# Gates and first key blocks as two threads, wider margins, and a solve whose loads are issued from two queues

## The chip, the cores and the metric

The kernel runs on one core of a Trainium2 chip, in one launch. Its time is what the device takes for it, in microseconds (us). A core has five engines with a queue of instructions each, worked off in order: TensorE (PE in the profile; its weight loads are PEld), VectorE (DVE), ScalarE (ACT), GpSimd (POOL) and SyncE (SP). SP and ACT also issue DMA transfers here (SPq and ACTq). An engine waits for another through semaphores. [...]

## What is computed

One layer of a hybrid model is applied to 128 context tokens and 512 latent tokens (640 in all, 2048 channels). With the parts that this change doesn't touch cut:

```
h    = rms_norm(x) * (1 + scale) + shift        # scale, shift from c @ w_mod
proj = h @ w_in                                 # u_f, z_f, q, k, v, z_d, a, b
y_f  = fft(u_f).real * silu(z_f)                # Fourier group
q, k, v = silu(short_conv(qkv))                 # 12 heads of 128
log_g = -exp(a_log) * softplus(a + dt_bias);  beta = sigmoid(b)     # the gates
per head, direction (2) and chunk of tokens:
  A    = I + strict_lower(beta * k @ k.T * exp(g_i - g_j))
  Tinv = triangular inverse of A
  scan over chunks:  v_new = Tinv @ (beta v - beta exp(g) k @ S)
                     o     = exp(g) q @ S + tril(q @ k.T * decay) @ v_new
                     S     = exp(g_last) S + (k * decay).T @ v_new
y = concat(y_f, rms_norm(o) * silu(z_d)) @ w_out;   out = rms_norm(x + gate * y)
```

Outputs are both token streams and the scan states of the context.

## The kernel before

**The stream.** The projection is cut into tiles of 128 output columns (53 of them in the main stream: u, k, v, q, z, f). Each tile is two halves of 320 tokens by 16 blocks of 128 channels, and each of these products is taken in three passes of rounded high and low parts (L1360: h_hi by whi, h_lo by whi, h_hi by wlo), so a tile is 96 matmuls. Weights come in as `raw` (issued by ACT, L1327), are rounded by ACT to `whi` (L1336), and POOL forms the rest `wlo` (L1344). At the end comes the output projection (L1628) in the same manner.

**The heads.** Beside the stream each of the 12 heads passes through generators: `conv` (L752 to L761 give KT, vT, QT), `blocks` (k transposed at L775 inside `to_tokens`; k times k at L841; the copies kkd at L846; the decays `gr`, loaded at L816 from gb4, L852 to L860; the store of `pd`, L863), `solve` (the 16x16 and 32x32 inverses of A on VectorE: loads NP, L875; steps L885, L887, L898, L900; store xd, L907; loads DD and DP, L912 and L915; a transpose L918; matmuls L929 and L940), `decay` (gb, L961; L973 to L980), `prep` (L1012, copy YT at L1014, L1025, L1040, L1047), `scan` (L1072 to L1125 and the squares L1137) and `head_out` (L1154). `gates` (L637 on) computes decays and betas of all heads once, from a load `abT`, and stores them to gd and gb4. `shifts` adds what the shift vector contributes: its last part (L617 and L620) runs over weight tiles wm that are loaded for it alone. `res_gates` forms column sums of two more weight groups on VectorE out of loads `gw` (L1258, steps L1264 and L1266 in `rows256`); the first two of these groups end in L1278.

**What sets the order.** The instructions are written in an order that a planner picks while the kernel is built. It keeps an estimate `est` of when each engine becomes free and when each tile is written, and all the generators above as threads with a rank. A thread stops at `yield`, and says when it wants to go on:

```
t = x.when + (GUARD if "P" in x.on else -LEAD)
return max([t] + [est.free[engine[e]] - SLACK for e in x.on if e != "P"])
```

`yield "P", t` goes on when TensorE's estimated time has reached t + 0.3, `yield "V"`, `"A"` or `"S"` when the thread's last result is due within 0.4 us and that engine is free within 0.9; a bare `yield` is "P" with the thread's own last end. `yield "poll"` waits until something is in the set `done`. In between, the stream's matmuls fill TensorE, two blocks of channels at a time, in the order of the list `names`; tile k or q of head h may only be finished once the scan of head h - 2 is done. The planner's times set the order alone; on the chip every engine runs as its semaphores let it.

`all_blocks` runs `gates()` first and then `blocks(0)`, `blocks(1)` and so on, as one thread.

Of the kernel before, what the change touches and what calls it, by code (L numbers as in the profile page):

```python
# [9 lines left out]
F32 = mybir.dt.float32  # L10
# [7 lines left out]
P = 128  # L18
# [194 lines left out]
def hybrid_step(ctx: ExitStack, tc: tile.TileContext, x_prompt, x_sample, state_ctx, c, c_ctx,  # L213
# [4 lines left out]
    est = Estimate()  # L218
# [26 lines left out]
    gb4 = dram.tile([NH, 4, 2, 160], F32, name="gb4")  # L245
# [332 lines left out]
    def shifts():  # L578
# [32 lines left out]
        for c in range(4):  # L611
            while len(sh_in) < n + 2:
                yield "poll"
            yield "P", max(est.written(x) for x in sh_in[n:n + 2]) + 1.7
            for j in range(4):
                x = sh_in[n + j // 2]
                PE.matmul(pc[32 * j:32 * j + 32, 0:384], lhsT=csh[:, 4 * c + j, :],  # L617
                          rhs=x[:, 0:768].rearrange("p (i n) -> p i n", i=3)[:, :, P * (j % 2):P * (j % 2) + P],
                          start=c == 0, stop=c == 3, tile_position=(0, 32 * j))
                PE.matmul(pa[32 * j:32 * j + 32, 0:48], lhsT=csh[:, 4 * c + j, :], rhs=x[:, 768 + 48 * (j % 2):816 + 48 * (j % 2)],  # L620
                          start=c == 0, stop=c == 3, tile_position=(0, 32 * j))
            n += 2
            sh_used[0] = n
# [13 lines left out]
    def gates():  # L637
# [20 lines left out]
        ACT.activation(beta, pbv[:, 24:48, :], AF.Tanh, scale=0.5)  # L658
        DVE.tensor_scalar(beta, beta, 0.5, 0.5, ALU.mult, ALU.add)
        DVE.tensor_scalar(nbeta, beta, -1.0, None, ALU.mult)  # L660
        DVE.tensor_scalar(aa, ax, -1.0, None, ALU.mult)
        DVE.tensor_tensor(aa, ax, aa, ALU.min)
        ACT.activation(aa, aa, AF.Exp)
# [147 lines left out]
    def blocks(h):  # L811
        s = st_h[h]
        KT = s["KT"]
        gr = g.tile([P, 2, 5, 32], F32, tag="gr", name="gr", bufs=1)
        for b in range(4):
            SP.dma_start(out=gr[32 * b:32 * b + 32].rearrange("p d t c -> p d (t c)"), in_=gb4[h, b].partition_broadcast(32))  # L816
        s["k"] = k = g.tile([P, 5, P], F32, tag="k", name="k", bufs=2)
        for sl, pv, n in to_tokens(KT):
            ACT.copy(k[:, sl, :], pv)
# [8 lines left out]
        rk2 = g.tile([P, 5], F32, tag="rk2", name="rk2", bufs=2)  # L828
        POOL.tensor_tensor(nk, sk, K("phalf")[:, 0:5], ALU.pow)
        DVE.reciprocal(rk2, sk)  # L830
        for nm, src in (("s3", beta4), ("ns3", nbeta4)):
            s[nm] = g.tile([P, 2, 5], F32, tag=nm, name=nm, bufs=3)
            DVE.tensor_tensor(s[nm], src[:, :, h, :], rk2.unsqueeze(1).broadcast_to([P, 2, 5]), ALU.mult)
# [14 lines left out]
        for b in range(4):  # L848
            POOL.memset(KK[32 * b:32 * b + 32, :, :, 32 * b:32 * b + 32], 0.0)
        done.add(("kk", h))  # L850
        sh = [P, 2, 5, 32]
        DVE.tensor_tensor(gr, gr, gg4[:, :, h, :].unsqueeze(3).broadcast_to(sh), ALU.subtract)  # L852
        DVE.tensor_tensor(gr, gr, dmask.unsqueeze(2).broadcast_to(sh), ALU.add)
# [14 lines left out]
    def solve(h):  # L868
# [3 lines left out]
        for b in range(4):  # L872
            for q in range(2):
                r = 32 * b + 16 * q
                SP.dma_start(out=NP[10 * b:10 * b + 10, 272 * q:272 * q + 256].rearrange("u (r c) -> u r c", r=16),  # L875
                             in_=pd[r:r + 16, :, :, 16 * q:16 * q + 16].rearrange("r d t c -> (d t) r c"))
        yield "V"
        tmp = g.tile([40, 768], F32, tag="tmp", name="tmp", bufs=1)
# [26 lines left out]
            yield "V" if q == 0 else "S"  # L905
        xd = dram.tile([40, 32, 32], F32, tag="xd", name="xd", bufs=2)
        SP.dma_start(out=xd, in_=X2)  # L907
        yield "S"
        while h and ("dd", h - 1) not in done:
            yield "poll"  # L910
        for b in range(4):
            SP.dma_start(out=DD[32 * b:32 * b + 32, 0:2].rearrange("p d t c -> p (d t) c"),  # L912
                         in_=xd[10 * b:10 * b + 10].rearrange("u r c -> r u c"))
            o = 32 * (b ^ 1)
            SP.dma_start(out=DP[o:o + 32], in_=xd[10 * b + 5:10 * b + 10].rearrange("u r c -> r u c"))  # L915
        yield "V", est.written(DD) + 1.5
        f2, N = "p d t c -> p (d t c)", s["N"]
        DVE.transpose(DD[:, 2:4].rearrange(f2), DD[:, 0:2].rearrange(f2))  # L918
        yield
        while h and ("prep", h - 1) not in done:  # L920
            yield "poll"

# [7 lines left out]
                              start=True, stop=True, tile_position=(32 * b, o))  # L930
        for j in range(2):
            ACT.copy(M2[:, j].rearrange(f1), px[j][:, 0:160])
        yield
        px = [bank(), bank()]
        for t in range(5):
            for j in range(2):
# [317 lines left out]
    def rows256(src, by):  # L1254
        x = g.tile([P, 4, 256], F32, tag="gw", name="gw", bufs=1)
        gw, acc = x[:, 0:2], x[:, 2:4]
        for j in range(NK // 2):
            SP.dma_start(out=gw, in_=src[:, 2 * j:2 * j + 2])  # L1258
            yield "V", est.last + 1.0
            for q in range(2):  # L1260
                for m in range(2):
                    one = by[:, 2 * j + q, m:m + 1]
                    if j + q:
                        DVE.scalar_tensor_tensor(acc[:, m], gw[:, q], one, acc[:, m], ALU.mult, ALU.add)  # L1264
                    else:
                        DVE.tensor_scalar(acc[:, m], gw[:, q], one, None, ALU.mult)  # L1266
        yield
        return x

    def shift_u():  # L1270
# [32 lines left out]


    place = {"k": C_K, "v": C_V, "q": C_Q, "z": C_ZD, "u": 0, "f": 512}
    names = "u0 u1 u2 u3 k1 q1 v1 z0 z1 f0".split()
    fill = {2: "", 3: "z2 f1", 11: "f2 z10 f3 z11"}
    for h in range(2, NH):
        names += [f"k{h}", f"v{h}", f"q{h}"] + fill.get(h, f"z{h - 1}").split()
    tiles = [(n[0], int(n[1:]), place[n[0]] + P * int(n[1:])) for n in names]  # L1310
# [8 lines left out]
    def loads():  # L1319
        for n, parts in enumerate(jobs):  # L1320
            while n >= len(ready) // 2 + 2:
                yield "poll"
            if n > 1:
                yield "A", est.freed(raws[n - 2])
            raw = wpool.tile([P, 8, P], F32, tag="raw", name="raw", bufs=2)
            for sl, src in parts:
                ACT.dma_start(out=raw[:, sl].rearrange("p a b -> p (a b)") if len(parts) > 1 else raw, in_=src)  # L1327
            raws.append(raw)

    def casts():  # L1330
        for c in range(2 * len(jobs)):
            while c >= 2 * len(raws) or c >= used[0] + 5:
                yield "poll"
            yield "A", max(est.written(raws[c // 2]), est.freed(his[c - 5]) if c > 4 else 0.0)
            his.append(wpool.tile([P, 4, P], F32R, tag="whi", name="whi", bufs=5))
            ACT.copy(his[c], raws[c // 2][:, 4 * (c % 2):4 * (c % 2) + 4])  # L1336
# [94 lines left out]
    fconst = []  # L1431

    def all_blocks():
        yield from gates()
        for h in range(NH):
            while ("k", h) not in done:
                yield "poll"
            yield from blocks(h)
            done.add(("blocks", h))
# [7 lines left out]

    def decays():
        for h in range(NH):
            while not {("v", h), ("q", h), ("kk", h)} <= done:  # L1450
                yield "poll"
            yield from decay(h)
            yield
            done.add(("decay", h))
# [204 lines left out]
    main, tail = stream(), out_stream()  # L1659
    est.free.update(PE=13.0, Activation=8.0, DVE=8.0, Pool=5.0, SP=0.0)  # L1660
    nc.push_inst_callback(est)
    for rank, steps in ((0, loads()), (0, casts()), (0, lows()), (2.4, solves()), (2.2, all_blocks()), (2, scans()), (3, outs()), (4, preps()), (5, decays()),
                        (2.5, fouriers(0)), (2.5, fouriers(1)), (10, res_gates()), (0.5, shift_loads()), (0.6, shifts()), (2.7, load_y(0)), (2.7, load_y(1))):
        begin(rank, steps)
    for i, kind in enumerate("kvq"):
# [41 lines left out]
```

## Time and profile before

| | |
|---|---|
| median of 3 runs | 1441.15 us (1438.79 to 1443.88) |
| the profiled execution | 1442.66 us, its span 1440.9 us |
| TensorE busy | 1373.0 us, 95% |
| TensorE weight loads | 1267.6 us, 88% |
| VectorE, ScalarE, GpSimd busy | 58%, 47%, 44% |
| mean granted TensorE clock | 0.982 |
| chain that ended last | TensorE 55%, VectorE 17%, DMA 4% of the span |

A share of busy time is a mean over stages. What an instruction waited for is read from the lists of waits and from the timeline, where the bracket behind a row gives the idle time before it and the engine and instruction that ended it.

### The profile page before, as it was taken

The numbers are of one execution on the slowest core, as the hardware profiler recorded it, in microseconds if no ns is written. First come the engines' busy times: TensorE is split into PE (matmuls) and PEld (weight loads), VectorE is DVE, ScalarE is ACT, GpSimd is POOL, SyncE is SP. The second block draws the span as 40 slices with busy tenths as digits, with TensorE's granted clock in tenths as the row PEclk, the third lists the DMA queues.
The fourth block names the chain that finished last, engine by engine and source line by source line (L and its number), as shares of the span: only waits on it lengthen the run. The fifth ranks groups of instructions, "written<-read, shape, count | busy, mean of one in ns | idle before, by whom it ended". The sixth has DMA issues, their size and how long they took to land.

```text
span 1440.9 us, 31437 instructions
## 1 busy us (share of the span) xinstructions
PE 1373.0 (95%) x12284; PEld 1267.6 (88%) x12284; DVE 842.6 (58%) x1756; ACT 670.8 (47%) x1808; POOL 628.4 (44%) x649
## 2 busy tenths in 40 slices
PE   6999989888999999999999999999999999999996
PEld 4799869887999999898999999998989998888884
DVE  5441127878597858586685969676755635322024
ACT  5332226644555464544455564645555544423134
POOL 2233213353355455354453545444454432346375
PEclk9999999898999999999999999999999999999998
DMA  9988973353344434334443424433333445594003
GB/s 311 277 262 265 309 191 106 95 144 100 90 129 116 117 101 127 103 110 124 117 125 101 127 79 133 120 113 113 97 93 88 137 138 164 172 338 147 30 0 146
DMA packets 271057, 203.71 MB, mean 141 GB/s; under 512 B 55801, under 2 KB 241094, under 8 KB 270782
## 3 DMA queue, kind: packets, MB, share of 16 engines
q1 hardware_dynamic: 148286, 129.88, 29.3%
q10 hardware_dynamic: 122624, 71.84, 17.5%
q8 instruction: 97, 1.59, 0.4%
q14 instruction: 50, 0.41, 0.1%
HBM read 177.67 MB, written 23.99 MB: 140 GB/s over the span
## 4 chain that ended last, share of the span: by engine, by line
PE 55%; DVE 17%; DMA 4%; ACT 2%; issue 2%; SPq 2%; POOL 1%; ACTq 0%; DVEq 0%; POOLq 0%
PE mbank L1360 28%; PE bank L1628 8%; PE mbank L1628 7%; DVE tmp L898 3%; DVE gw L1264 3%; DVE tmp L885 2%; PE bank L1091 1%; PE bank L1111 1%; PE bank L1099 1%; PE bank L1072 1%; DMA DD<-xd 1%; PE bank L1079 1%; DVE XB L887 1%; PE bank L841 1%; DVE YB L900 1%
## 5 line engine op out<-in xcount | busy, mean ns | idle before, releaser
L1360 PE MATMUL mbank<-h_hi,whi 128*128 128x320 f32 (+1 forms) x1696 | 554.3, 327 | 0.0
L1344 POOL TENSOR_TENSOR wlo<-raw,whi 128x512 fp32r<-128x512 f32 x232 | 329.6, 1426 | 506.8 <-ACT whi L1336 452.2
L1360 PE MATMUL mbank<-h_lo,whi 128*128 128x320 f32 (+1 forms) x1696 | 528.3, 311 | 0.0
L1360 PE MATMUL mbank<-h_hi,wlo 128*128 128x320 f32 (+1 forms) x1696 | 528.0, 311 | 0.1
L1360 PEld LDWEIGHTS mbank<-h_hi,whi 128*128 128x128 f32 x1696 | 322.5, 190 | 10.7 <-issue 7.4
L1360 PEld LDWEIGHTS mbank<-h_lo,whi 128*128 128x128 f32 x1696 | 322.7, 190 | 0.1
L1360 PEld LDWEIGHTS mbank<-h_hi,wlo 128*128 128x128 f32 x1696 | 322.2, 190 | 0.3 <-POOL wlo L1344 0.3
L1336 ACT CAST whi<-raw 128x512 fp32r<-128x512 f32 x232 | 142.2, 618 | 195.2 <-PE mbank L1360 141.6
L1264 DVE SCALAR_TENSOR_TENSOR gw<-gw,cz 128x256 f32<-128x256 f32 x240 | 130.6, 602 | 5.6 <-DMA gw<-in_w_mod 5.4
L283 POOL TENSOR_TENSOR wlo<-raw,whi 128x512 fp32r<-128x512 f32 (+1 forms) x44 | 55.3, 1267 | 86.8 <-ACT whi L282 64.9
L1628 PE MATMUL mbank<-wlo,y_hi 128*128 128x512 f32 x160 | 63.8, 399 | 2.6 <-POOL wlo L283 2.0
L1628 PE MATMUL mbank<-whi,y_hi 128*128 128x512 f32 x160 | 64.1, 401 | 0.0
L1628 PE MATMUL mbank<-whi,y_lo 128*128 128x512 f32 x160 | 64.0, 400 | 0.0
L1628 PE MATMUL bank<-whi,y_lo 128*128 128x512 f32 x160 | 63.2, 395 | 0.0
L1628 PE MATMUL bank<-wlo,y_hi 128*128 128x512 f32 x160 | 63.1, 394 | 0.0
L1628 PE MATMUL bank<-whi,y_hi 128*128 128x512 f32 x160 | 62.9, 393 | 0.0
L1094 ACT ACTIVATE vn<-bank,s 128x128 f32<-128x128 f32 x120 | 37.6, 366 | 50.0 <-PE bank L1091 49.5
L977 ACT ACTIVATE E<-gb,ngg 128x128 f32<-128x128 f32 x120 | 41.7, 396 | 32.6 <-DVE AT L980 25.4
L282 ACT CAST whi<-raw 128x512 fp32r<-128x512 f32 (+1 forms) x44 | 24.6, 579 | 56.4 <-PE bank L1628 19.1
L965 POOL TENSOR_TENSOR gb<-gb,cst 128x640 f32<-128x640 f32 x24 | 37.0, 1558 | 27.7 <-DMA gb<-gd 27.7
L1084 POOL TENSOR_SCALAR kd<-k,edl 128x128 f32<-128x128 f32 x96 | 46.4, 497 | 1.1 <-PE bank L1099 0.7
L1106 DVE SCALAR_TENSOR_TENSOR S<-S,egl,bank 128x128 f32<-128x128 f32 x72 | 21.6, 339 | 37.9 <-PE bank L1099 35.8
(334 smaller groups left out, 2452.6 us busy)
## 6 DMA issues: line engine op xcount, KB each, us to landing
raw<-in_w_in ACTq DMA_DIRECT2D x106, 512.0 KB
wm<-in_w_mod SPq DMA_DIRECT2D x64, 512.0 KB
gw<-in_w_mod SPq DMA_DIRECT2D x64, 256.0 KB
raw<-in_w_out ACTq DMA_DIRECT2D x48, 256.0 KB
gb<-gd SPq DMA_DIRECT2D x12, 640.0 KB
yd<-zs SPq DMA_DIRECT2D x16, 320.0 KB
yt<-yd SPq DMA_DIRECT2D x16, 320.0 KB
out<-res SPq DMA_DIRECT2D x10, 512.0 KB
```

The source lines that it names most:

```text
L283: sub.tensor_tensor(wlo, raw_part, whi, ALU.subtract)
L885: DVE.tensor_tensor(tv, NPd[:, :, i, 0:i].unsqueeze(2).broadcast_to(s4), Xd[:, :, 0:i, 0:i].rearrange("p h j c -> p h c j"), ALU.mult)
L898: DVE.tensor_tensor(tv, A.unsqueeze(2).broadcast_to(s4), B.rearrange("p j c -> p c j").unsqueeze(1).broadcast_to(s4), ALU.mult)
L965: POOL.tensor_tensor(gv, gv, masks[d].unsqueeze(1).broadcast_to([P, 5, P]), ALU.add)
L977: ACT.activation(E[:, 1 - d], gb[:, d, P * t:P * (t + 1)], AF.Exp, bias=ngg4[:, d, h, t:t + 1])
L1084: POOL.tensor_scalar(kd[:, d], k[:, tt[d], :], edl4[:, d, h, tt[d]:tt[d] + 1], 1.0, ALU.mult, ALU.mult)
L1094: ACT.mul(vn[:, d], pv[:, P * d:P * (d + 1)], s["s3"][:, d, tt[d]:tt[d] + 1])
L1264: DVE.scalar_tensor_tensor(acc[:, m], gw[:, q], one, acc[:, m], ALU.mult, ALU.add)
L1336: ACT.copy(his[c], raws[c // 2][:, 4 * (c % 2):4 * (c % 2) + 4])
L1344: POOL.tensor_tensor(lo, raws[c // 2][:, 4 * (c % 2):4 * (c % 2) + 4], his[c], ALU.subtract)
L1360: PE.matmul(pm[:, 0:b - a], lhsT=w, rhs=h[k][:, a:b], start=k + m == 0, stop=k == NK - 1 and m == 2)
L1628: PE.matmul(acc[t], lhsT=a[kk][:, sl], rhs=w, start=kk == order[0] and j == 0, stop=kk == order[-1] and j == 2)
```

## The change

The gates become a thread of their own with rank 1.8, and the first head's key blocks no longer wait for them as a whole: `blocks(0)` waits for `beta` where it is used, and loads gr only once the gates are stored. Decays now wait for the gates as well. Five margins of the planner change: the shift product (1.7 to 3.5), the end of `rows256` (an added 3.0), and in the solve 0.5 ahead of L929, DP's landing plus 1.0 ahead of L940, and "AS" with the landing of xd ahead of DD. Half of the NP loads and half of the DD loads are issued by ACT, and all four DD loads are issued ahead of the DP loads. In the stream, f1 moves from behind z2 of head 3 to behind f0.

```diff
@@ shifts
-            yield "P", max(est.written(x) for x in sh_in[n:n + 2]) + 1.7
+            yield "P", max(est.written(x) for x in sh_in[n:n + 2]) + 3.5
@@ gates
+        done.add("beta")
@@ blocks
-        gr = g.tile([P, 2, 5, 32], F32, tag="gr", name="gr", bufs=1)
-        for b in range(4):
-            SP.dma_start(out=gr[32 * b:...], in_=gb4[h, b].partition_broadcast(32))
+        def decays_in(): ...          # the same four loads
+        gr = decays_in() if h else None
...
+        while "beta" not in done:
+            yield "poll"
...
         done.add(("kk", h))
+        if not h:
+            while "gates" not in done:
+                yield "poll"
+            yield "S"
+            gr = decays_in()
+            yield "V", [gr]
@@ solve
-                SP.dma_start(out=NP[10 * b:10 * b + 10, ...], in_=pd[r:r + 16, ...])
+                (ACT if q else SP).dma_start(out=NP[10 * b:10 * b + 10, ...], in_=pd[r:r + 16, ...])
...
-        yield "S"
+        yield "AS", est.last
...
         for b in range(4):
-            SP.dma_start(out=DD[32 * b:32 * b + 32, 0:2]..., in_=xd[10 * b:10 * b + 10]...)
+            (ACT if b % 2 else SP).dma_start(out=DD[32 * b:32 * b + 32, 0:2]..., in_=xd[10 * b:10 * b + 10]...)
+        for b in range(4):
             o = 32 * (b ^ 1)
             SP.dma_start(out=DP[o:o + 32], in_=xd[10 * b + 5:10 * b + 10]...)
...
-        yield
+        yield "P", est.last + 0.5                                   # ahead of L929
...
-        yield
+        yield "P", max(est.last, est.written(DP) + 1.0)             # ahead of L940
@@ rows256
-        yield
+        yield "P", est.last + 3.0
@@ the stream's list
-    names = "u0 u1 u2 u3 k1 q1 v1 z0 z1 f0".split()
-    fill = {2: "", 3: "z2 f1", 11: "f2 z10 f3 z11"}
+    names = "u0 u1 u2 u3 k1 q1 v1 z0 z1 f0 f1".split()
+    fill = {2: "", 11: "f2 z10 f3 z11"}
@@ all_blocks, decays, threads
-        yield from gates()
-            while not {("v", h), ("q", h), ("kk", h)} <= done:
+            while not {("v", h), ("q", h), ("kk", h), "gates"} <= done:
+    ... (1.8, gates()), (2.2, all_blocks()) ...
```

Lines behind the change have other numbers in the changed kernel: L816 becomes L819, L863 L877, L875 L889, L907 L921, L912 L926, L915 L930, L961 L976, L1014 L1029, L1025 L1040, L1137 L1152, L1258 L1273, L1360 L1375.

SyncE's queue from the store of the gates to the first solve's loads, before:

```order
L693 DMA gd<-gT 24x640
L698 DMA gb_72<-gT_2565 48x1x160 x2
L816 DMA gr<-gb_72 32x320 x4
L1258 DMA gw<-in_w_in 128x2x256 x3
L961 DMA gb<-gd 128x2x640
L1258 DMA gw<-in_w_in 128x2x256
L863 DMA pd<-g_2829 128x320
L816 DMA gr<-gb_72 32x320 x4
L875 DMA NP<-pd 10x16x16 x8
```

and the same place now:

```order
L694 DMA gd<-gT 24x640
L1273 DMA gw<-in_w_in 128x2x256
L699 DMA gb_72<-gT_2567 48x1x160 x2
L1273 DMA gw<-in_w_in 128x2x256
L976 DMA gb<-gd 128x2x640
L819 DMA gr<-gb_72 32x320 x4
L1273 DMA gw<-in_w_in 128x2x256 x2
L877 DMA pd<-g_2871 128x320
L819 DMA gr<-gb_72 32x320 x4
L889 DMA NP<-pd 10x16x16 x4
```

The loads of gr for head 0 moved behind two weight loads and the load of gb; the eight NP loads became four, and four more stand in ScalarE's queue.

SyncE's queue at the end of the solve of head 4, before (the pair of DD and DP stands four times):

```order
L907 DMA xd<-XB 40x1024
L799 DMA yd_80<-zs 128x640
L1258 DMA gw<-in_w_mod 128x2x256
L912 DMA DD<-xd 32x10x32
L915 DMA DP<-xd 32x5x32
```

and now:

```order
L921 DMA xd<-XB 40x1024
L1273 DMA gw<-in_w_mod 128x2x256
L926 DMA DD<-xd 32x10x32 x2
L930 DMA DP<-xd 32x5x32 x4
L800 DMA yd_80<-zs 128x640
```

The other two DD loads of that solve stand in ScalarE's queue, between a load of stream weights and the exponentials of the decays:

```order
L792 ACTIVATE zs<-pj_1297 128x512
L1342 DMA raw<-in_w_in 128x8x128
L926 DMA DD<-xd 32x10x32 x2
L992 ACTIVATE E<-gb,ngg 128x128 x8
L1351 CAST whi<-raw 128x512
```

ScalarE's queue had no load of a solve before; the DD loads moved there keep their place in the solve.

ScalarE's queue in `prep` of head 1, while head 0's scan ends, before (vn is the scan's, jk the squares of its output):

```order
L1094 ACTIVATE vn<-bank,s_2726 128x128 x2
L988 ACTIVATE jq<-QT 128x128
L989 ACTIVATE jq<-QT 128x512
L1137 ACTIVATE jk,m<-o 128x128 x5
L1014 COPY YT<-bank 128x160
L1033 COPY KK<-bank 32x5x32 x4
L1042 COPY ET<-bank 128x320
```

and now:

```order
L1351 CAST whi<-raw 128x512
L1109 ACTIVATE vn<-bank,s_2656 128x128 x2
L1029 COPY YT<-bank 128x160
L1048 COPY KK<-bank 32x5x32 x4
L1057 COPY ET<-bank 128x320
L1152 ACTIVATE jk,m<-o 128x128 x5
```

The copies of `prep` moved ahead of the five squares.

## Rows read from the trace of the kernel before

**Rows 1.** The profile's page, busy time, share of the span and instructions of engines.

```profile
PE 1373.0 (95%) x12284; PEld 1267.6 (88%) x12284; DVE 842.6 (58%) x1756; ACT 670.8 (47%) x1808; POOL 628.4 (44%) x649
```

**Rows 2.** TensorE's waits: line, what ended them, us in total, times, longest.

```profile
PE bank L929 <- DVE DD L918: 9.7, 7, 3.3
...
PE bank L1278 <- DVE gw L1264: 7.1, 2, 6.6
PE bank L940 <- issue: 4.9, 4, 1.9
PE bank L617 <- DMA wm<-in_w_in: 4.6, 3, 2.8
...
PE bank L1025 <- ACT YT L1014: 3.4, 1, 3.4
PE bank L1072 <- DVE S L1106: 2.8, 2, 1.7
```

**Rows 3.** Stretches: length, busy us by engine, granted clock, DMA share, GB/s.

```profile
256.00:272.00 16.00, 9.38 (x49) 9.11 (x49) 13.37 (x34) 8.37 (x26) 4.81 (x4) 0.68 0.35 94
...
346.00:360.00 14.00, 10.17 (x114) 9.44 (x114) 8.49 (x24) 5.87 (x20) 3.28 (x5) 0.63 0.30 100
...
584.00:592.00 8.00, 5.91 (x170) 4.85 (x171) 4.40 (x8) 2.06 (x5) 1.27 (x1) 0.79 0.51 156
```

**Rows 4.** Chain that ended last, 275 to 293 us: start, us, what.

```profile
275.72 15.95 PE mbank L1360 x108
```

**Rows 5.** Timeline, shift product, SyncE and TensorE: start, us, instruction, [idle before].

```profile
195.78 7.49 SPq L574 DMA_DIRECT2D wm<-in_w_in  x13
...
207.65 1.46 PE L617 MATMUL bank<-wm,csh 128*32 128x384 f32 x4 [2.76 <-DMA wm<-in_w_in]
```

**Rows 6.** Timeline of TensorE and VectorE, gates and first L1278.

```profile
224.00 0.40 PE L673 MATMUL bank<-ab,cst 128*128 128x60 f32 x2 [0.43 <-DVE ab L670]
224.41 0.83 DVE L761 SCALAR_TENSOR_TENSOR KT<-th,KT 128x641 f32<-128x641 f32 x1 [0.56 <-ACT th L759]
...
259.23 1.44 DVE L859 TENSOR_TENSOR gr<-gr,kkd 128x160 f32<-128x160 f32 x1
...
262.21 1.62 DVE L1264 SCALAR_TENSOR_TENSOR gw<-gw,csh 128x256 f32<-128x256 f32 x4
...
263.49 1.87 PE L1278 MATMUL bank<-cst,gw 128*128 128x1 f32 x8 [6.62 <-DVE gw L1264]
```

**Rows 7.** Timeline of SyncE, VectorE and TensorE, end of head 4's solve.

```profile
578.02 0.41 SPq L912 DMA_DIRECT2D DD<-xd  x1
...
581.12 3.71 DVE L1264 SCALAR_TENSOR_TENSOR gw<-gw,cz 128x256 f32<-128x256 f32 x4
581.98 0.38 SPq L912 DMA_DIRECT2D DD<-xd  x1
582.40 0.46 SPq L915 DMA_DIRECT2D DP<-xd  x1
...
585.53 0.51 DVE L918 STREAM_TRANSPOSE DD<-DD 128x320 f32<-128x320 f32 x1 [0.70 <-DMA DD<-xd]
586.09 0.89 PE L929 MATMUL bank<-DD,g 32*32 32x32 f32 x80 [3.34 <-DVE DD L918]
```

**Rows 8.** Timeline of SyncE and ScalarE, start of head 7's solve.

```profile
778.54 0.35 SPq L863 DMA_DIRECT2D pd<-g  x1
...
782.47 3.62 SPq L875 DMA_DIRECT2D NP<-pd  x8
783.62 0.62 ACT L1336 CAST whi<-raw 128x512 fp32r<-128x512 f32 x1 [3.78 <-PE mbank L1360]
```

**Rows 9.** Timeline of ScalarE and TensorE, head 1's prep.

```profile
349.07 0.27 ACT L1014 COPY YT<-bank 128x160 f32<-128x160 f32 x1
...
349.40 0.76 PE L1025 MATMUL bank<-DD,YT 32*32 32x32 f32 x40 [3.39 <-ACT YT L1014]
```

**Rows 10.** Tile DD, its loads: count, duration min, median, max in ns, first and last start.

```profile
L912 SPq DMA_DIRECT2D DD<-xd x48: 303/386/1676, 289.8 to 1129.5; - x48
```

More of the change, by code (lines that the diff above doesn't have):

```diff
@@ L813, in blocks, with decays_in @@
         KT = s["KT"]
-        gr = g.tile([P, 2, 5, 32], F32, tag="gr", name="gr", bufs=1)
-        for b in range(4):
-            SP.dma_start(out=gr[32 * b:32 * b + 32].rearrange("p d t c -> p d (t c)"), in_=gb4[h, b].partition_broadcast(32))
+        def decays_in():
+            x = g.tile([P, 2, 5, 32], F32, tag="gr", name="gr", bufs=1)
+            for b in range(4):
+                SP.dma_start(out=x[32 * b:32 * b + 32].rearrange("p d t c -> p d (t c)"), in_=gb4[h, b].partition_broadcast(32))
+            return x
+        gr = decays_in() if h else None
         s["k"] = k = g.tile([P, 5, P], F32, tag="k", name="k", bufs=2)
@@ L874, in solve @@
                 r = 32 * b + 16 * q
-                SP.dma_start(out=NP[10 * b:10 * b + 10, 272 * q:272 * q + 256].rearrange("u (r c) -> u r c", r=16),
+                (ACT if q else SP).dma_start(out=NP[10 * b:10 * b + 10, 272 * q:272 * q + 256].rearrange("u (r c) -> u r c", r=16),
                              in_=pd[r:r + 16, :, :, 16 * q:16 * q + 16].rearrange("r d t c -> (d t) r c"))
@@ L911, in solve @@
         for b in range(4):
-            SP.dma_start(out=DD[32 * b:32 * b + 32, 0:2].rearrange("p d t c -> p (d t) c"),
-                         in_=xd[10 * b:10 * b + 10].rearrange("u r c -> r u c"))
+            (ACT if b % 2 else SP).dma_start(out=DD[32 * b:32 * b + 32, 0:2].rearrange("p d t c -> p (d t) c"),
+                                             in_=xd[10 * b:10 * b + 10].rearrange("u r c -> r u c"))
+        for b in range(4):
             o = 32 * (b ^ 1)
@@ L1661, in hybrid_step @@
     nc.push_inst_callback(est)
-    for rank, steps in ((0, loads()), (0, casts()), (0, lows()), (2.4, solves()), (2.2, all_blocks()), (2, scans()), (3, outs()), (4, preps()), (5, decays()),
+    for rank, steps in ((0, loads()), (0, casts()), (0, lows()), (2.4, solves()), (1.8, gates()), (2.2, all_blocks()), (2, scans()), (3, outs()), (4, preps()), (5, decays()),
                         (2.5, fouriers(0)), (2.5, fouriers(1)), (10, res_gates()), (0.5, shift_loads()), (0.6, shifts()), (2.7, load_y(0)), (2.7, load_y(1))):
```

## The prediction

> **What bounds the kernel now.** I read the busy times first. TensorE is busy for 1373.0 of 1440.9 us, 95% [rows 1], and both kernels issue the same matmuls (5088 in the projection stream, in the same three-pass batches), so nothing can be won but TensorE's idle time and the time it spends at the lower of its two clock levels. The next view is the list of what TensorE waited for [rows 2]: the largest waits are for the solve's transposed blocks (L929, 9.7 us in 7 waits), the column weights of the Fourier shift (L1278, 7.1 us), a part of the solve that the profile calls issue (L940, 4.9 us), the loads of the shift product (L617, 4.6 us) and one copy on ScalarE (L1025, 3.4 us). Third comes the clock by stage [rows 3]. [...] What the clock takes is the stretch times what is missing from 1: 16 x 0.32 = 5.1 us, 14 x 0.37 = 5.2 us, and 8 x 0.21 = 1.7 us twice (the second such stretch, at 984, reads alike). [...]
>
> **Gates and key blocks as threads, and L1278.** The gates' own instructions stay. Head 0's key transposes (L775) move ahead of the gates' last transposes on TensorE, right behind L673 to L675. That adds a wait: VectorE finishes KT at 224.41 + 0.83 = 225.24, while L673 starts at 224.00 [rows 6] and its group of three is short; the price is 0 to 1.2 us, I take 0.5. Behind it in TensorE's queue stands the stream, which nobody waits for there. On SyncE the four loads of gr now stand behind two weight loads and the load of gb; their cover is that the key blocks must first be ready, and pd of head 0, which needs gr, now has 5.6 us more of TensorE's work ahead of it in the order (the matmuls counted).
>
> The gain here is another one. The shift's column sums (L1278) waited because the eighth weight tile is worked on by VectorE only at 262.21, behind two multiplies of 1.44 us that begin at 259.23 [rows 6]. Counted in the order of instructions, 162 stream matmuls stand between the gates' transposes (L689) and L1278 before, and 246 after, because f1 fills and because L1278 is placed with a margin of 3 us more. 84 more at 15.95/108 = 0.148 us [rows 4] are 12.4 us, against a wait of 6.6 us. The weight loads themselves keep their number and order, so I expect the wait gone, and with it the clock's 5.1 us: 11.7 us at most, nothing at least (if VectorE is later by as much). I take -10, the 0.5 for KT and 1.2 for a rest of the clock included.
>
> **The margin of the shift product (L617): 0.** SyncE issues 13 of its loads back to back, 7.49 us from 195.78 on, and the last tile's wait ends at 207.65 [rows 5]. In the new order twelve stream matmuls move from behind the second group to ahead of it; ahead of the fourth group stands as much work as before. The last load is late by the same amount, and the 4.6 us come in one piece instead of three. Ends: -1.8 (twelve matmuls) and +1; I take 0.
>
> **The solve's loads.** In head 4 the first DD load is issued at 578.02 and the fourth at 581.98, with the DP loads between; the transpose starts at 585.53 and TensorE has waited 3.34 us when it starts at 586.09 [rows 7]. With two DD loads on each queue and DP behind them, the last DD load goes out one issue of 0.386 us [rows 10] after the first, not 3.96 us after. That is 3.6 us in this head; with four gaps of 0.45 us and none longer it would be some 2.3 us. The largest of the seven waits is 3.3 us and their mean 1.4, and the plan adds 0.5 us ahead of L929. I take 8.7 of 9.7 us away. The DP loads are still within four issues of SyncE, and L940 now has a margin of 1 us where its longest wait was 1.9: 2.3 of 4.9 us. Together -11, ends 0 and -14.6. Two of the clock's stretches follow such waits, 3.4 us: I take -2.5.
>
> **Head 1.** At 349.07 ScalarE copies YT, and TensorE had waited 3.39 us for it [rows 9]; in the order this copy stands behind the five squares of head 0's output (L1137), which wait for VectorE. In the new order it stands ahead of them. What is late next: in the new order L1027, L1040, L1055 and L1062 follow without stream matmuls between them, where before L1278 and L1154 covered two of the bounces. I price those at 1.5 us, three to four times the 0.33 us from the copy to its matmul plus the matmul's own start. Of the clock's 5.2 us I take half: -3.4 + 1.5 - 2.6 = -4.5, ends -8.6 and +3.
>
> **What the change adds on ScalarE.** 12 x (4 NP + 2 DD) = 72 issues at some 0.38 us are 27 us of its time. ScalarE waits where the landing is not there yet. In head 7 pd is issued at 778.54 and the first NP load only at 782.47; ScalarE was idle for 3.78 us up to 783.62 [rows 8], so here the wait would be free and the four issues would delay the cast behind them by under 1 us. Behind such an issue stand the raw loads, the casts of the stream and vn; whoever waits for those is TensorE. Of its waits before, only L1025 is put down to ScalarE [rows 2], so there is cover. Ends 0 and +27; near the row of head 7 I take +5.
>
> **Waits that move.** TensorE's waits are also time in which the others catch up. L1072 (2.8 us) shows where the next one sits. I give back a good quarter of the 14.6 us: +4, ends 0 and +10.
>
> **Sum.** -10 - 11 - 2.5 - 4.5 + 5 + 4 = -19.0. The profiled execution took 1442.66 us (span 1440.9 and 1.8 around it), which gives 1423.7; it is 1.5 above the median of the runs, 1441.15, so 1422.
>
> **The rivals.**
> First, the loads gain little (18%). If a solve is late because xd lands late, or because VectorE is busy (four column steps from 581.12 on end just before the transpose could start), two queues don't help: -3 in place of -13.5, 1433. Against it: SyncE needs 4.8 us for the eight issues, more than the 3.55 us from the last DD issue to the transpose [rows 7]. [...]
>
> Second, slower (17%): ScalarE is held. Its queue is in order, and an NP or DD issue that comes before pd or xd has landed keeps vn and the casts back. There are 24 such places; SyncE was held 3.9 us at one of them [rows 8]. It decides from (19 + 5)/24 = 1 us per place that reaches TensorE; at 1.25 us it is 30 in place of 5, 1447. For it: xd and pd are on the path of every head. Against it: the plan asks for ScalarE only once it reckons the DMA landed, and ScalarE's idle time was not filled. [...]
>
> Third, all of it goes (13%): 11.7 + 14.6 + 3.4 + 8.6 = 38.3 us and nothing is given back, 1403. Against it: waits seldom go without successors.
>
> **How the numbers follow.** The forecast has 52%, by itself 1411 to 1431. A measurement of this kernel can tell some 0.3%, 4.3 us, from no change. Faster: nearly all of the forecast (0.50), two thirds of the first rival (0.12), the third (0.13), so 0.75. Same: 0.11 from the edges of the first three cases. Slower: 0.14, nearly all from the second. The range 1404 to 1440 leaves out most of the second rival and half of the third's lower side.
>
> **What would show it.** L1278's first wait gone and the clock of its stretch near 1; L929 under 2 us in total; DD's last issue within 1 us of its first; YT ahead of the squares; L617 still 4 to 5 us. Wrong if waits of TensorE for vn, whi or wlo grow beyond 10 us (the second rival), or if L929 keeps over 5 us (the first).

## The result: slower by 0.7%, and the profile after

The changed kernel takes 1449.95 us (median of 5 runs, 1448.25 to 1451.62), the kernel before in the same rounds 1441.15 (1438.44 to 1444.26): ratio 1.0068, 95% interval 1.0048 to 1.0088. Forecast were 1422 us with an upper end of 1440, so sign and range were wrong. The profiled execution took 1448.9 us, with a span of 1447.1 against 1440.9: 6.2 us of the 8.8 between the medians show in these two traces.

The page's first part, as in [rows 1]:

```profile
PE 1378.5 (95%) x12284; PEld 1272.6 (88%) x12284; DVE 845.9 (58%) x1756; ACT 669.6 (46%) x1808; POOL 636.3 (44%) x649
```

TensorE is busy for 5.5 us more with the same 12284 matmuls, and the span is 6.2 us longer. So nearly all of what the traces show of the loss lies in matmuls that took longer, and TensorE's idle time is the same to 0.7 us. Its list of waits, against [rows 2]:

```profile
PE bank L944 <- DVE DD L933: 14.2, 7, 3.9
...
PE bank L776 <- DVE KT L762: 4.4, 2, 3.1
...
PE bank L617 <- DMA wm<-in_w_in: 3.5, 2, 2.8
PE bank L1009 <- ACT add L769: 2.4, 1, 2.4
PE bank L651 <- ACT abT L531: 2.3, 1, 2.3
PE mbank L1642 <- ACT y_hi L1527: 2.0, 1, 2.0
PE bank L1169 <- DVE o L1158: 2.0, 1, 2.0
```

L1293 (L1278 of before), L955 (L940) and the copy YT (L1025 of before) have left the list: 15.4 us of waits gone, as forecast. The wait ahead of the solve's first matmuls (L944, L929 before) rose from 9.7 to 14.2 us, though 8.7 of it was to go, and others are new or longer, five of them by 1.6 to 3.9 us. Granted clock by stretch, in the columns of [rows 3] (the number behind POOL's is the clock): first the three stretches shown there, then three others.

```profile
256.00:272.00 16.00, 16.00 (x116) 15.99 (x115) 14.01 (x31) 8.72 (x27) 6.88 (x5) 1.00 0.41 109
346.00:360.00 14.00, 10.42 (x154) 9.38 (x154) 9.87 (x23) 7.88 (x26) 5.58 (x10) 0.76 0.32 97
584.00:592.00 8.00, 8.00 (x164) 6.93 (x164) 5.41 (x14) 3.02 (x8) 4.44 (x9) 0.84 0.59 180
...
296.00:304.00 8.00, 6.93 (x179) 6.52 (x180) 3.70 (x7) 2.31 (x7) 1.50 (x2) 0.57 0.57 152
...
579.00:587.00 8.00, 6.34 (x178) 5.88 (x179) 6.20 (x16) 3.37 (x9) 4.28 (x4) 0.57 0.58 174
668.00:676.00 8.00, 6.43 (x178) 6.08 (x179) 7.93 (x19) 3.56 (x9) 1.27 (x1) 0.57 0.56 166
```

The stretch at the first L1278 went from 0.68 to 1.00, as hoped. But three waits for the solve of 2.84, 3.92 and 3.87 us (heads 0, 4 and 5) come each with a stretch of 6.8 us at a granted clock of 0.50; this and 1.00 are the only two levels in the two traces. Over the whole span the lower level was granted for 61.8 us, against 51.8 before. Reckoned as in the prediction, the stretch times what is missing from 1, half of the difference, 5.0 us, is lost to the clock; that is most of TensorE's longer work.

Head 4 shows the solve's new end. The timeline's rows (start, us, instruction, idle time before it and what ended it), against [rows 7]:

```profile
565.86 5.81 DVE L1279 SCALAR_TENSOR_TENSOR gw<-gw,cz 128x256 f32<-128x256 f32 x4
571.70 0.37 SPq L1273 DMA_DIRECT2D gw<-in_w_mod  x1
572.25 1.09 SPq L926 DMA_DIRECT2D DD<-xd  x2
574.88 0.85 ACTq L926 DMA_DIRECT2D DD<-xd  x2
575.78 1.28 ACT L992 ACTIVATE E<-gb,ngg 128x128 f32<-128x128 f32 x4 [8.21 <-DMA DP<-xd]
576.51 0.42 DVE L994 TENSOR_TENSOR KK<-KK,E 128x256 f32<-128x256 f32 x1 [4.04 <-ACT E L992]
580.10 0.50 DVE L933 STREAM_TRANSPOSE DD<-DD 128x320 f32<-128x320 f32 x1
580.66 1.09 PE L944 MATMUL bank<-DD,g 32*32 32x32 f32 x80 [3.92 <-DVE DD L933]
```

xd landed at 567.15. SyncE was held until 571.70 at a gw load, which waits for the four column steps of VectorE (5.81 us here); the two DD loads behind it went out from 572.25. ScalarE issued its own two only at 574.88 and 575.36, and its engine was idle for 8.21 us up to 575.78. In the trace the two carry the semaphores 107 and 108, as SyncE's two DD loads do, and those landed at 574.81 and 575.34, just ahead of them. So the two queues did not run side by side here. Behind ScalarE's issues stood E (L992), for which VectorE waited 4.04 us, and behind that the transpose.

Head 5 is another case. DD's last load landed at 663.6, and the transpose began 5.4 us later: it stood in VectorE's queue behind a wait for E and four column steps:

```profile
665.44 1.06 DVE L994 TENSOR_TENSOR KK<-KK,E 128x256 f32<-128x256 f32 x1 [4.10 <-ACT E L992]
666.42 0.41 DVE L995 TENSOR_TENSOR AT<-bank,E 128x256 f32<-128x256 f32 x1
666.75 2.34 DVE L1279 SCALAR_TENSOR_TENSOR gw<-gw,cz 128x256 f32<-128x256 f32 x4
669.01 0.50 DVE L933 STREAM_TRANSPOSE DD<-DD 128x320 f32<-128x320 f32 x1
```

In the mean of the 12 heads DD's last landing came 6.4 us after xd's (7.1 before): under 4 us in heads 1, 3 and 11, over 10 in heads 2, 4 and 7. From there to the transpose it took 2.4 us on average, where before it was 0.8. So what the loads gained, 0.7 us, VectorE's queue took twice over.

The mean hides two kinds of heads. In five heads no gw load stands in SyncE's queue between xd and DD's last load: there the landing came 3.6 us after xd's, where in the five such heads of before it was 5.9. In the seven others it came 8.5 us after, before 8.0. So the loads gained 2.3 us where nothing stood in their way, and nothing elsewhere; and all but 0.4 of the 14.2 us of waits lie in the seven heads with a gw load (before 7.3 of 9.7). From the first to the last issue of DD's four loads it is 2.6 us in the mean, 3.2 before, and under 1 us in four heads only.

VectorE's groups (count, busy us, mean ns, idle us before and what ended it), the column steps and the product with E, of before:

```profile
L1264 DVE SCALAR_TENSOR_TENSOR gw<-gw,cz 128x256 f32<-128x256 f32 x240 | 130.6, 602 | 5.6 <-DMA gw<-in_w_mod 5.4
L979 DVE TENSOR_TENSOR KK<-KK,E 128x256 f32<-128x256 f32 x60 | 34.0, 567 | 3.0 <-ACT E L977 2.7
L1264 DVE SCALAR_TENSOR_TENSOR gw<-gw,csh 128x256 f32<-128x256 f32 x60 | 30.6, 567 | 9.6 <-DMA gw<-in_w_in 9.6
```

and of the changed kernel:

```profile
L1279 DVE SCALAR_TENSOR_TENSOR gw<-gw,cz 128x256 f32<-128x256 f32 x240 | 141.9, 649 | 16.5 <-DMA gw<-in_w_mod 16.4
L1279 DVE SCALAR_TENSOR_TENSOR gw<-gw,csh 128x256 f32<-128x256 f32 x60 | 39.9, 722 | 10.5 <-DMA gw<-in_w_in 10.5
...
L994 DVE TENSOR_TENSOR KK<-KK,E 128x256 f32<-128x256 f32 x60 | 31.8, 530 | 15.1 <-ACT E L992 11.6 <-ACT add L769 3.4
```

These 300 steps cost 20.6 us more, and VectorE waits 8.9 us more for ScalarE's E. VectorE's whole busy time rose by 3.3 us only, since other steps became shorter; but column steps now stand in VectorE's queue between DD's landing and the transpose in eight heads, before in three.

### The profile page after: what moved, and what is told of

It is laid out like the page before. It is cut to its first block, busy times and chain, and to the rows that moved or that the text cites. A ratio compares the mean times of both kernels' runs of the same rounds, so it can differ in the third digit from the quotient of the medians.

```text
span 1447.1 us, 31425 instructions
## 1 busy us (share of the span) xinstructions
PE 1378.5 (95%) x12284; PEld 1272.6 (88%) x12284; DVE 845.9 (58%) x1756; ACT 669.6 (46%) x1808; POOL 636.3 (44%) x649
## 5 line engine op out<-in xcount | busy, mean ns | idle before, releaser
L1375 PE MATMUL mbank<-h_hi,whi 128*128 128x320 f32 (+1 forms) x1696 | 556.8, 328 | 0.0
L1375 PE MATMUL mbank<-h_hi,wlo 128*128 128x320 f32 (+1 forms) x1696 | 529.6, 312 | 0.6 <-POOL wlo L1359 0.5
L1375 PE MATMUL mbank<-h_lo,whi 128*128 128x320 f32 (+1 forms) x1696 | 529.6, 312 | 0.0
L1375 PEld LDWEIGHTS mbank<-h_hi,whi 128*128 128x128 f32 x1696 | 323.6, 191 | 10.6 <-issue 7.3
L1375 PEld LDWEIGHTS mbank<-h_hi,wlo 128*128 128x128 f32 x1696 | 323.3, 191 | 1.6 <-POOL wlo L1359 1.6
L1375 PEld LDWEIGHTS mbank<-h_lo,whi 128*128 128x128 f32 x1696 | 323.9, 191 | 0.3
L1279 DVE SCALAR_TENSOR_TENSOR gw<-gw,cz 128x256 f32<-128x256 f32 x240 | 141.9, 649 | 16.5 <-DMA gw<-in_w_mod 16.4
L1642 PE MATMUL mbank<-wlo,y_hi 128*128 128x512 f32 x160 | 64.5, 403 | 2.6 <-POOL wlo L283 2.0
L1642 PE MATMUL mbank<-whi,y_hi 128*128 128x512 f32 x160 | 64.2, 402 | 2.0 <-ACT y_hi L1527 2.0
L1642 PE MATMUL mbank<-whi,y_lo 128*128 128x512 f32 x160 | 64.4, 403 | 0.1
L1642 PE MATMUL bank<-whi,y_hi 128*128 128x512 f32 x160 | 63.2, 395 | 0.0
L1642 PE MATMUL bank<-wlo,y_hi 128*128 128x512 f32 x160 | 63.2, 395 | 0.0
L1642 PE MATMUL bank<-whi,y_lo 128*128 128x512 f32 x160 | 63.2, 395 | 0.0
L992 ACT ACTIVATE E<-gb,ngg 128x128 f32<-128x128 f32 x120 | 41.2, 395 | 40.7 <-DVE AT L995 10.2
L1279 DVE SCALAR_TENSOR_TENSOR gw<-gw,csh 128x256 f32<-128x256 f32 x60 | 39.9, 722 | 10.5 <-DMA gw<-in_w_in 10.5
```

Of the source, the lines that this page charges most:

```text
L992: ACT.activation(E[:, 1 - d], gb[:, d, P * t:P * (t + 1)], AF.Exp, bias=ngg4[:, d, h, t:t + 1])
L1375: PE.matmul(pm[:, 0:b - a], lhsT=w, rhs=h[k][:, a:b], start=k + m == 0, stop=k == NK - 1 and m == 2)
L1642: PE.matmul(acc[t], lhsT=a[kk][:, sl], rhs=w, start=kk == order[0] and j == 0, stop=kk == order[-1] and j == 2)
```

## The experiments

Ratios are to the kernel before, timed in the same rounds on the same chip, with their 95% intervals. The kernels come from several chips, so they are compared with each other by these ratios and not by the medians. "Solve waits" are TensorE's ahead of the solve's first matmuls, from the profiled execution.

| kernel | median us | ratio | solve waits us |
|---|---|---|---|
| the change | 1449.95 | 1.0068 (1.0048 to 1.0088) | 14.2 |
| solve_old | 1441.73 | 0.9990 (0.9973 to 1.0007) | 11.4 |
| gates_old | 1471.79 | 1.0210 (1.0175 to 1.0246) | 12.5 |
| same_order_sp | 1453.17 | 1.0075 (1.0047 to 1.0102) | 6.9 |
| margin2 | 1446.83 | 1.0028 (1.0012 to 1.0045) | 3.4 |
| margin4 | 1437.04 | 0.9955 (0.9933 to 0.9976) | 0 |
| margin6 | 1440.68 | 0.9986 (0.9971 to 1.0001) | 0 |
| before_m4 | 1455.26 | 1.0103 (1.0083 to 1.0122) | 0 |
| solve_old_m4 | 1433.24 | 0.9948 (0.9930 to 0.9967) | 0 |
| gates_old_m4 | 1461.15 | 1.0120 (1.0096 to 1.0145) | 3.7 |
| gw_hold | 1448.26 | 1.0051 (1.0033 to 1.0069) | 8.0 |
| gw_small | 1422.16 | 0.9845 (0.9820 to 0.9869) | 2.6 |
| dd_when_sp | 1457.27 | 1.0088 (1.0058 to 1.0118) | 10.3 |
| same_order_act | 1444.21 | 1.0009 (0.9990 to 1.0028) | 9.8 |
| same_order_act_m4 | 1445.83 | 1.0018 (0.9998 to 1.0038) | 0 |
| shift_margin | 1442.73 | 1.0014 (0.9998 to 1.0030) | 11.7 |
| placebo | 1476.31 | 1.0223 (1.0191 to 1.0256) | 15.2 |
| placebo_b80 | 1447.86 | 1.0053 (1.0030 to 1.0076) | 19.0 |
| placebo_a | 1449.64 | 1.0065 (1.0040 to 1.0090) | 2.4 |

**The change in two halves.** solve_old takes the solve's hunk of the diff back; gates_old applies that hunk alone to the kernel before.

> The changed kernel with the solve of before (all loads on SyncE, DD and DP in turn, no added margins); the threads of gates and first key blocks, the margins of the shift product and of rows256 and f1's new place stay. Theory A (the solve's edits cost: its loads are late because SyncE is held by a gw load, and its transpose stands behind VectorE's other work): the wait at L1293 stays gone and the sum of waits ahead of the solve's first matmuls is near the 9.7 us of before, so 1425 to 1438 us. Rival B (the threads cost: waits for KT, abT and the product q k that are new): 1445 us or more.

> The kernel before with all of the solve's edits and nothing else of the change. Theory A: the wait at L1278 is back (about 7 us and its stretch at the low clock), the solve's waits are 12 us or more, 1446 to 1458 us. Rival B: 1425 to 1438 us, with the solve's waits under 6 us.

The threads, margins and f1 alone change nothing that can be measured (forecast: 1425 to 1438); L1293's wait stays gone, but waits come elsewhere. The solve's edits alone cost 2.1%, more than in the change as a whole and more than the 1446 to 1458 us expected. So the loss came with the solve's half, if with one. Each half also has a new order, and the last group of experiments shows what that moves by itself.

**The margin ahead of the solve's first matmuls.** Three kernels and the change make a row for it: 0.5, 2, 4 and 6 us.

```diff
-        yield "P", est.last + 0.5
+        yield "P", est.last + 4.0      # margin2: 2.0, margin6: 6.0; so too in gates_old_m4
```

> The changed kernel with 4.0 us in place of 0.5 ahead of the solve's first matmuls, so that more of the stream stands ahead of them on TensorE. Theory A: the waits there fall from 14.2 us to under 4, and four of the half-speed stretches that follow them go (each 3.4 to 6.8 us long, so 1.7 to 3.4 us each): 1430 to 1440 us. Rival C (a wait of TensorE that goes only moves to the next one, since the other engines use it to catch up): sum of waits as now, 1446 to 1453 us.

> The changed kernel with 2.0 us ahead of the solve's first matmuls (0.5: 1450 us; 4.0: 1437 us). Theory A, a straight effect of the margin: in between, 1440 to 1446 us, waits there 4 to 9 us. Theory D (each margin gives another order, and its time scatters by 10 us): outside of 1437 to 1450 us, or waits there that don't fall.

> The changed kernel with 6.0 us ahead of the solve's first matmuls. Theory A: no waits there, as with 4.0, and the heads end 2 us later each, which nobody waits for: 1432 to 1441 us. Theory D: outside of that.

> The kernel before with a margin of 4.0 us ahead of the solve's first matmuls and nothing else. Theory A: its 9.7 us of waits there go, with the two half-speed stretches that follow them (3.4 us each): 1426 to 1436 us. Rival C (waits move): 1438 us or more.

> The changed kernel with the solve of before (all loads on SyncE), and 4.0 us ahead of its first matmuls. If two queues for the loads are worth something once TensorE no longer waits there: 1440 us or more. If they are worth nothing (theory A): as the changed kernel with the same margin or below it, 1428 to 1437 us.

> The kernel before with all of the solve's edits, and 4.0 us in place of 0.5 ahead of the solve's first matmuls. If the 0.5 is what made the solve's edits slow (1471.8 us without this): its 12.5 us of waits and the low clock behind them go, 1440 to 1455 us. If it is the order that the planner happens to write (theory D; the same margin made the kernel before slower, 1455.3 us): 1460 us or more.

With 4 us the solve waits are gone and the changed kernel is 1.1% faster, and 0.45% faster than before. In head 5 of margin4 the transpose is as late as ever, and nobody waits for it (timeline; L944 has no bracket, so no idle time):

```profile
655.05 3.75 DVE L1279 SCALAR_TENSOR_TENSOR gw<-gw,cz 128x256 f32<-128x256 f32 x4
658.72 0.50 DVE L933 STREAM_TRANSPOSE DD<-DD 128x320 f32<-128x320 f32 x1
...
661.29 0.89 PE L944 MATMUL bank<-DD,g 32*32 32x32 f32 x80
```

The row of margins has the ratios 1.0068, 1.0028, 0.9955 and 0.9986. For 4 and 6 us this is as expected; margin2 lies just above its range, with smaller waits than expected (3.4 us in place of 4 to 9). solve_old_m4 (the change without its solve edits, and 4 us) and margin4 are the best kernels here that compute everything, and can't be told apart: 0.9948 and 0.9955. In gates_old_m4 the margin took back 0.9 of the 2.1% of gates_old, with 3.7 us of solve waits in place of 12.5; 1461 us is in the range of the new order, not in that of the thin margin. And the same margin made the kernel before 1% slower, against an expectation of 1426 to 1436, although its solve waits went as well. That contradicts a straight gain.

**The queues, with the order kept.** In these three the planner reckons the loads where they were, so TensorE, VectorE and GpSimd have their instructions in the same order (as the change, as solve_old and as solve_old_m4), and the issuing engine alone differs.

```diff
+                est.alias = "Activation" if q else None     # what the planner reckons with
-                (ACT if q else SP).dma_start(out=NP[...
+                SP.dma_start(out=NP[...                     # DD alike; same_order_act: the other way round
```

> The changed kernel, all instructions in the same order on TensorE, VectorE and GpSimd, but the NP and DD loads that ScalarE issues are issued by SyncE (the planner reckons them on ScalarE still, so that nothing else moves). The rival of the prediction (ScalarE is held at its issues, 1447 us): with the 72 issues gone ScalarE's casts and copies are free, 1430 to 1441 us. Theory A: SyncE is the one that is held, its place in the order has not moved, and eight issues in a row cost 1 to 2 us more per head: 1447 to 1458 us, waits at the solve's first matmuls 14 us or more.

> The changed kernel with the solve of before (1441.7 us), every instruction in the same place, but half of the NP and DD loads are issued by ScalarE (the planner reckons them on SyncE, so that nothing else moves; DD and DP stay in turn). By the prediction two queues take 2 to 4 us from each solve's path, and TensorE's 11.4 us of waits ahead of its first matmuls fall by two thirds: 1430 to 1436 us. By theory A (the loads don't set the end, VectorE's queue does): within 0.3% of 1441.7 us, waits above 8 us. By the rival of the prediction (ScalarE held at its issues): 1447 us or more.

> The same issue by two queues in the kernel with the solve of before and 4.0 us ahead of its first matmuls (1433.2 us). TensorE does not wait there any more, so theory A expects nothing: 1430 to 1437 us. ScalarE held: 1440 us or more.

SyncE alone against both queues: 1.0075 and 1.0068; 0.9990 and 1.0009; 0.9948 and 1.0018. Two queues gain nothing that can be told in the first two pairs, and cost 0.7% in the third, where the kernel was to stay at 1430 to 1437. There TensorE waits for ScalarE's results:

```profile
PE bank L1119 <- ACT vn L1114: 5.2, 3, 2.0
PE bank L1045 <- ACT YT L1034: 3.6, 1, 3.6
...
PE bank L1014 <- ACT jq L1009: 2.4, 2, 1.8
```

In same_order_sp DD's four loads go out within 1.6 us in the mean, faster from one queue than the 2.6 us from two. The solve waits are half of those of the change (14 or more were expected), and VectorE waits 1.2 us for E in place of 11.6:

```profile
L1000 DVE TENSOR_TENSOR KK<-KK,E 128x256 f32<-128x256 f32 x60 | 31.0, 516 | 3.2 <-ACT add L771 1.8 <-ACT E L998 1.2
```

So ScalarE was held, as the second rival said. Yet the time did not come back: other waits took the place, 4.1 us for the loads of S and 2.9 us for zl among them. The run puts the 72 issues on SyncE instead, so it weighs one hold against the other; what ScalarE's alone costs it does not show.

**VectorE's and SyncE's gw work.** gw_hold keeps the gw loads and steps out of the stretch from xd to the transpose; gw_small keeps the order of the change word for word and makes these loads and steps 8 columns wide, so that the modulation is not computed in full; dd_when_sp takes the new wait away.

```diff
+            while held:                                   # gw_hold, ahead of load and steps
+                yield "poll"
-            SP.dma_start(out=gw, ...)                      # gw_small
+            SP.dma_start(out=gw[:, :, 0:8], ...)
-        yield "AS", est.last                               # dd_when_sp
+        yield "S"
```

> The changed kernel, in which the gate weights' loads gw (SyncE) and their column steps (VectorE) are not written into the order while a solve is between its store xd and its transpose. The margin ahead of the solve's first matmuls stays 0.5. Theory A (the loads are late because SyncE is held by a gw load and the transpose stands behind VectorE's column steps): DD's last load lands within 3.5 us of xd's landing in all but one or two heads, the waits ahead of the solve's first matmuls fall from 14.2 us to under 6, 1434 to 1444 us. Rival C (the margin alone is too thin, whatever is in the queues): waits there stay above 10 us, 1446 us or more.

> The changed kernel in the very same order on every engine, margins too, but of each group of eight gw loads all behind the first carry 8 of 256 columns, and VectorE's column steps behind the first work on 8 columns (the planner is told the old sizes). So the modulation of this part is not computed. Theory A (SyncE is held ahead of DD by a gw load that waits for VectorE's column steps, and the transpose stands behind those steps): with the order as it is, DD's last load lands within 3 us of xd's landing in 10 heads or more, the waits ahead of the solve's first matmuls fall from 14.2 us to under 4 us, 1425 to 1438 us. Rival (the order on TensorE is too tight by itself, whatever VectorE and SyncE carry): those waits stay at 8 us or more, 1442 us or more.

> The changed kernel, in which DD's loads are written into the order when SyncE is free by the plan, without waiting for ScalarE and for xd's reckoned landing as well. If the added wait is the edit that let the solve slip behind gw loads: waits ahead of the solve's first matmuls under 8 us, 1436 to 1443 us. Theory A as it stands now (VectorE's queue and the thin margin, this edit or not): 10 us or more there, 1446 to 1454 us.

gw_small is the clearest run: same order, same margins, and the solve waits fall to 2.6 us.

```profile
PE bank L949 <- DVE DD L938: 2.6, 2, 1.5
```

One half of its expectation failed: DD's last load lands within 3 us of xd in two heads only, in place of ten, with a mean of 5.7 us. From xd's landing to the transpose it is 7.5 us on average, in the change 8.8; half of that comes from an earlier landing (SyncE is held for less) and half from VectorE's shorter queue. So in this order the gw work makes the solve late on both ways. VectorE's waits for E are as long as in the change (11.8 us), so they alone don't make TensorE wait. The 28 us can't be had by an edit, since 97 us of VectorE's work are left out (300 steps, 85.0 in place of 181.8 us). gw_hold has a new order, and missed its expectation: 8.0 us at the solve, and 6.0 us in one wait for KT. From xd's landing to the transpose it is 6.2 us on average, less than in gw_small, so this time alone does not set the waits either; when TensorE comes by its order counts too. DD's last load landed within 3.5 us of xd in four heads, not in ten or more. In head 7 ScalarE's queue kept it back, at a cast that waited for raw weights, 6.7 us behind SyncE's first DD load (799.50), and TensorE waited 3.0 us:

```profile
806.16 0.62 ACT L1359 CAST whi<-raw 128x512 fp32r<-128x512 f32 x1 [5.02 <-DMA raw<-in_w_in]
806.17 0.33 ACTq L927 DMA_DIRECT2D DD<-xd  x1
```

dd_when_sp is no better than the change (in its order a gw load stands between xd and DD in eight heads, in the change's in seven and in that of before also in seven), so the added wait was not what put gw loads there.

**What a new order moves by itself.** shift_margin is one edit of the change. The placebos alter the planner's price for a change of matmul kind, which has no reason to help or harm.

```diff
-                d += 85
+                d += 90        # placebo (before), placebo_a (the change); 80 in placebo_b80 (before)
```

> The kernel before with the margin of the shift product alone raised from 1.7 to 3.5 us. By the prediction's term: 0, with ends of -1.8 and +1, so 1439 to 1444 us. If any edit that makes the planner write another order behind it moves the time by several us (theory D: a part of every difference here is that), then outside of that, up or down by 4 us or more.

> The kernel before, in which the planner reckons 90 ns in place of 85 for TensorE's change from one kind of matmul to another, and nothing else: another order of the same instructions, by no reason. What it moves is what any new order moves. If differences of a per cent need a reason: within 0.3% of before. If not (theory D): off by 0.4% or more, up or down.

> The kernel before with 80 ns in place of 85 in the same place. If before is one order among many of like time: on either side of 1441 us. If its order is an unusually good one, as the first such kernel (90 ns, 1476 us) suggests: 1450 us or more again.

> The changed kernel, in which the planner reckons 90 ns in place of 85 for TensorE's change from one kind of matmul to another, and nothing else. If the changed kernel's time belongs to its edits: within 0.3% of its own 1450 us. Theory D (any new order of the planner moves the time by a per cent): 1435 us or less, or 1460 us or more.

The price of the shift's margin was 0, as forecast; as far as the trace shows, it moves twelve matmuls of the stream ahead of the shift product's second group and nothing else of TensorE. Of the two nonsense edits of the kernel before one costs 2.2%, the other 0.5%, and the solve's wait grows in both (15.2 and 19.0 us, longest 5.7 and 5.3):

```profile
PE bank L929 <- DVE DD L918: 15.2, 4, 5.7
```

```profile
PE bank L929 <- DVE DD L918: 19.0, 7, 5.3
```

The second is between its two expectations, at 1447.9 us: slower than before, but not by as much as the first. The changed kernel's neighbour stays at 1449.6, with solve waits of 2.4 us and 5.1 us for o (L1169) in their place.

## Why the prediction was wrong

- **L1278:** right. The waits of 7.1 us and the low clock behind the first are gone, and in gates_old they are back (6.6 us).
- **L617:** right in size, 4.6 to 3.5 us; shift_margin agrees with 0.
- **L940 and head 1's YT:** the waits went, 4.9 us (2.3 forecast) and 3.4 us. In head 1 some two thirds of the 4.5 us came: L1055 and L1062 now wait 0.94 and 1.21 us, and the clock of that stretch is 0.76, so that 1.7 us of the forecast 2.6 came back there.
- **The solve's loads, -11:** the step that failed. It read the DD issues, 3.96 us apart, as what the transpose waits for, let the last one go out 0.386 us after the first, and put the gain straight onto TensorE. Measured, L929 went from 9.7 to 14.2 us in place of 1.0. Two things were wrong in it. The two queues did not run side by side: from DD's first issue to its last it is 2.7 to 5.4 us in the seven heads with a gw load, and head 4 shows SyncE held at that load until 571.70 and ScalarE's two issues right behind the landings of SyncE's (574.88 behind 574.81, 575.36 behind 575.34). And the issues were one of two things that end close together; the other, four column steps from 581.12 on, stood in the same rows [rows 7] and was given to the first rival. The transpose stands behind VectorE's queue for 3.8 to 5.4 us after DD has landed in heads 1, 3, 5 and 8, of which 5 and 8 made TensorE wait. The 2.3 us that the prediction had as its smaller gain did come in the five heads without a gw load, but only 2.3 of the 9.7 us of waits lay in such heads. gw_small shows, with the order unchanged, that without the gw work these waits go (14.2 to 2.6 us); same_order_sp shows that ScalarE's issues have a part in them too (6.9 us). Two queues for one show no gain, by the pairs above.
- **The clock, -9.0 in all:** became +5.0. That a wait that goes takes its stretch at the lower clock with it was the author's estimate. The forecast had -5.1 and a rest of 1.2 at L1278, -2.6 in head 1 and -2.5 at the solve. The first two came in the main; but behind the solve's waits of 2.4 to 3.9 us in heads 0, 4, 5 and 7 there are now 23.9 us at a granted clock of 0.50, in place of 6.8 us at the solve before: +8.5 us in place of -2.5. Two more such stretches, 10.2 us, stand at the waits of L1009 with L1169 and of L1642. A wait of 3.09 us for KT (L776, at 424) has none, so not every wait of this length brings one.
- **Waits that move, +4:** measured at some 12 us (L776, L1009, L651, L1642, L1169 grew by 3.9, 2.4, 1.6, 2.0 and 2.0) with another 5.1 us of clock at L1009, L1169 and L1642.
- **ScalarE, +5:** the mechanism of the second rival is there (E, same_order_sp), and its 1447 us is nearest of all. Moving the issues back brought no time back, but put them on SyncE; so what this term is worth by itself stays open. The prediction also took only L1025 of TensorE's waits for ScalarE's; the whole list of before has 3.8 us for h_hi (L430) and 0.5 to 0.7 us for vn and abT as well. The first rival had the right reason, VectorE, and its sign came (L929 over 5 us), but it had the wrong time, since it had no term for VectorE getting later.

Added up from the two traces: L1278 -12.2 us with its clock, head 1 -2.9, L617 -1.1, the solve +8.1 (4.5 and 8.5, less the 4.9 of L940), the waits that moved +17.0 with their clock; with -1.7 of clock in the first 40 us, that is +7.2, and smaller differences bring it to the 6.2 us of the spans.

What the prediction did not have at all: the margins, names and waits are inputs of a planner, and each writes a new order behind the edit. The sum of 19 us was set against a kernel whose neighbours by nonsense edits are 0.5 and 2.2% slower, so a loss of about the measured size comes without any reason of the change's own. Whether the solve's edits cost 0.7% by themselves, or whether this order is an ordinary one and that of before a lucky one, stays open: three neighbours of before, one of them nearly the same order, and one of the change are too few, and before_m4 against margin4 says that an edit's sign depends on the rest of the order. It speaks for a fortunate order of before that both nonsense edits made it slower, and for a loss of the change's own that its neighbour stayed at 1.0065.

## What to carry to other kernels

A late instruction can have more than one queue in front of it, as the transpose of head 4 had here (SyncE's to 571.70, ScalarE's to 574.88, VectorE's to 580.10): before pricing a shorter one, look at what would be next on the engine that does the waiting step. Where a planner orders the work by estimates, try slack ahead of the matmuls that read another engine's result (here 4 us helped three orders by 0.4 to 1.1% and cost the fourth 1.0%), and judge an edit against a few neighbours of the kernel made by edits without sense. An experiment that keeps the order and changes one engine or one size (planner told the old one) says more than one that takes an edit back.

## What was not expected of the hardware

- Most column steps of VectorE take either some 0.48 us or some 1.51 us (the two medians). Of the 300, 32 were over 0.9 us before, and 53 in the changed kernel; in 52 of these 53 GpSimd was at work when the step began, in 46 of them on a wlo, which takes 1.43 us in the mean; among the other 247 GpSimd was at work in 49, in 6 of them on a wlo. In gw_small, of the steps of 8 columns 30 still take over 0.9 us (median 1.30, the others 0.22), and in 28 of them GpSimd was at work when the step began. So a slow step takes some 1.0 us more at 256 columns and 1.1 us more at 8. Why slow steps and GpSimd's work go together was not shown; a run without GpSimd's work was not made. The planner reckons 0.54 us always.
- Over the profiled executions of all kernels here, span less TensorE's idle time less half of its time at a granted clock of 0.50 is 1344 to 1353 us, while the spans go from 1416 to 1476. So idle time and clock are nearly all there is to win or lose here.
